# One more Strassen unit in the last gate pair, a shorter lead at its end, other accumulator banks for two groups, and another place for the last two quarter transposes of x1

## The chip, the cores and the metric

The kernel runs on one core of a Trainium2 chip. It is one launch that computes one decoder layer for 256 tokens. The metric is the device time of that launch in microseconds (us), the median over several runs, each of them one execution.

## The reference, cut to what matters

```python
h = rmsnorm(x, norm_mix_g);  u = h @ w_in              # D = 2048, 256 tokens
c_g, b_g, xa, za, q, fl, iv, og, ga, gb = split(u)
ya = b_g * causal_dwconv3(c_g * xa, conv_w) * silu(za)
o  = hgrn2_chunked(silu(q), (1 - lb) * sigmoid(-fl), iv, log_f)
yb = o * lax.rsqrt(mean(o * o) + EPS) * hg_norm_g * silu(og)
m  = sigmoid(ga) * (ya @ w_a_out) + sigmoid(gb) * (yb @ w_b_out)
x  = x + m @ w_o
gate = sigmoid(rmsnorm(x, ple_norm_g) @ w_ple_gate)    # 2048 x 2048
x  = x + gate * (p @ w_ple_proj)
return rmsnorm(x, final_norm_g)
```

All operands are fp32. The change touches the product with `w_o`, the product with `w_ple_gate` (`w_pg` in the kernel), and one scaling in the HGRN2 branch.

## The kernel before

**Products.** The 256 tokens are two halves `t` of 128 (`NT`), and the contraction of 2048 is 16 blocks of 128 (`KT`). An fp32 operand is split in two parts, hi and lo, and a product is three matmuls: hi by hi, hi by lo, lo by hi. A weight chunk of two blocks by 512 columns is one *step*. `split` (lines 143 to 173) writes the hi part of a step's weights on ScalarE (`whi`, L166) and the lo part on VectorE (`wlo`, L167), 128x1024 each, and the matmuls of the step then use them. A full step is 12 matmuls of 128x512 (L1258, or L1280 where two groups are a pair). The raw weights come on the queue of SP (`raw`, 3 buffers, 1 MB each). The split parts live in a ring of ten.

**Groups.** A group is 512 output columns. The stages run in this order: the projections with `w_in`, the merge gates, then `w_o` (a pair `OO` with columns 0 and 1, then `O` with j = 2 and j = 3), then `w_pg` (`PG0`, the pair `GP` with groups 1 and 2, then the last group, `PG3`). A pair follows a *program*, a tuple of units. The unit `(0, c)` takes group 0 at chunks c and c + 1, `(1, c)` the same for group 1, `(2, c)` takes chunk c for both groups (two steps, 8 products), and `("S", c)` takes chunk c for both groups by Strassen's form: 7 products, 4 steps. Three of these steps split 128x1024 and one 128x512, the latter from `t2`. After the first step of such a unit `combine_weights` (L181, L184, L185, VectorE) makes its sums of weights in place. `forms` makes the matching sums of the activations. The banks of a pair are put together by `sums` (L845), which for `GP` feeds `gated` (L1014 sigmoid on ScalarE; L1017 `t*pw` and L1018 `xs+t` on VectorE; L1026 a multiplication by `gfin_t` on GpSimd).

**The turn of x1.** When a group of `w_o` is done, `ep_o` adds it to the residual (L845, `xs`), copies it into another order on ScalarE (L947), and has it transposed by `turned`: four DMA writes to DRAM (L346, `turn<-t`), one DMA read (L350, `t<-turn`), then, `lag` steps later in the program, a 32x32 transposition on VectorE (L354). For the quarters j = 2 and 3 `put` then splits it into `xh` (ScalarE, L310, four instructions) and `xl` (VectorE, L311, four). Quarter j = 3 is chunks 6 and 7 of every product with `w_pg`. `lag` is 6 for j = 1 and otherwise 2.

**Order.** Each engine works through its instructions in the order of its own list. A scheduler makes the lists from the order in which the program issues the instructions and from what they depend on, with `issue_after` as a hint and `keep_in_program_order` to hold an instruction. The splits are issued `ahead(pos)` steps before the matmuls that use them; from the last stage on this lead grows from 3 by one every 3 steps, to 8 at most (line 1251). Epilogues are generators, of which `advance` takes one `yield` at each step. The positions in `tied` get an `issue_after` on the split before.

**Banks.** PSUM has four banks with the tag `g` and four with the tag `s`. A plain group uses two `g` banks, a pair four `g` and four `s`.

**The end.** The last group (from line 1446) does its half t = 0 with 128x512 matmuls, and t = 1 twice with 128x256; all its splits are issued during t = 0.

The program of the last pair:

```python
LATE = (0, 4), ("S", 0), (0, 6), ("S", 1), (2, 3), ("S", 2), (1, 4), (1, 6)
```

## Time and profile before

| | us |
|---|---|
| median of 3 runs (808.6 to 808.78) | 808.68 |
| the profiled execution, its own time | 809.07 |
| its span, first to last instruction | 807.3 |
| PE busy | 798.0 (99%) |
| VectorE (DVE) busy | 685.1 (85%) |
| ScalarE (ACT) busy | 492.1 (61%) |
| GpSimd (POOL) busy | 95.4 (12%) |
| mean granted clock of TensorE | 0.996 |

A row of the timeline has the start in us, the duration in us, the engine, the line, the operation, output<-inputs by the program's names, partitions x elements and type, and the number of instructions put together in the row; in brackets stands the idle time ahead of it and what ended it. Matmuls overlap: the duration of one is longer than the distance to the next, which is 0.2266 us for a 128x512 fp32 matmul here, so time lost on PE is read from the starts. SPq is the queue of SP. The timeline cuts the names of tiles shorter than the lists of instructions below do: `t` is `t4_...` or `t2_...`, `xl` is `xl_1039`.

### The profile page before, as it was taken

To read this page: it belongs to the slowest core of one execution; us is meant where nothing else is said; L and a number is where in the kernel's file an instruction comes from. 1 tells how busy PE (TensorE), PEld (TensorE's weight loads), DVE (VectorE), ACT (ScalarE), POOL (GpSimd) and SP (SyncE) were. 2 spreads that over 40 slices of the span, in tenths; PEclk is the share of its full clock that TensorE was granted. 3 is DMA by queue.
4 is the path that set the end of the run, shared out by engine and by line. 5 is a ranking of instruction groups with operands and counts; after the bars stand their busy time and mean duration, and the time that the engine had idled before them with its cause. 6 is when DMAs were issued, how large, how long until landed. Compare 5 with 4: busy or idle time off the path is not lost.

```text
span 807.3 us, 11113 instructions
## 1 busy us (share of the span) xinstructions
PE 798.0 (99%) x4169; PEld 662.3 (82%) x4169; DVE 685.1 (85%) x798; ACT 492.1 (61%) x662; POOL 95.4 (12%) x74
## 2 busy tenths in 40 slices
PE   9999999999999999999999999999999999999995
PEld 7888888888888888888888888888888888887885
DVE  5968897966779987978998998998998988859995
ACT  6967565575656665586674564564565556746562
POOL 0000145300000054300001000000100000002032
PEclk9999999999999999999999999999999999999998
DMA  9899855747676755667584775775875669877542
GB/s 345 295 335 319 268 174 203 237 167 241 240 261 190 261 183 201 209 211 257 189 307 158 227 275 171 239 264 179 275 266 196 208 246 348 327 236 281 205 173 104
DMA packets 50309, 191.20 MB, mean 237 GB/s; under 512 B 5712, under 2 KB 15184, under 8 KB 36304
## 3 DMA queue, kind: packets, MB, share of 16 engines
q1 hardware_dynamic: 50112, 190.24, 68.4%
q8 instruction: 32, 0.52, 0.2%
q10 hardware_dynamic: 144, 0.26, 0.1%
q14 instruction: 21, 0.17, 0.1%
HBM read 175.80 MB, written 14.68 MB: 236 GB/s over the span
## 4 chain that ended last, share of the span: by engine, by line
PE 82%; DVE 10%; issue 2%; DMA 2%; ACT 2%; SPq 0%; POOL 0%; ACTq 0%; POOLq 0%; DVEq 0%
PE g L1258 48%; PE g L1280 25%; PE s L1280 6%; DVE wlo L167 5%; DMA raw<-in_w_pg 2%; ACT whi L166 1%; DVE raw L181 1%; DMA raw<-in_w_o 1%; PE s L1258 1%; PE s L504 1%; DVE t L845 1%; PE s L1131 1%; DVE t L184 1%; DVE t L1017 0%; DVE t L354 0%
## 5 line engine op out<-in xcount | busy, mean ns | idle before, releaser
L167 DVE TENSOR_TENSOR wlo<-raw,whi 128x1024 fp32r<-128x1024 f32 (+1 forms) x320 | 390.2, 1243 | 92.2 <-ACT whi L166 89.4
L166 ACT ACTIVATE whi<-raw 128x1024 fp32r<-128x1024 f32 (+1 forms) x320 | 325.8, 1047 | 175.8 <-PE g L1258 98.3
L1258 PE MATMUL g<-whi,xl 128*128 128x512 f32 (+1 forms) x464 | 177.1, 382 | 0.3 <-DVE xl L311 0.3
L1258 PE MATMUL g<-whi,xh 128*128 128x512 f32 (+1 forms) x464 | 177.4, 383 | 0.0
L1258 PE MATMUL g<-wlo,xh 128*128 128x512 f32 (+1 forms) x464 | 177.1, 382 | 0.0
L1280 PE MATMUL g<-whi,xl 128*128 128x512 f32 x316 | 122.9, 389 | 0.0
L1280 PE MATMUL g<-wlo,xh 128*128 128x512 f32 x316 | 122.9, 389 | 0.0
L1280 PE MATMUL g<-whi,xh 128*128 128x512 f32 x316 | 122.6, 389 | 0.0
L1258 PEld LDWEIGHTS g<-whi,xl 128*128 128x128 f32 x464 | 87.2, 188 | 17.6 <-DVE xl L311 0.8
L1258 PEld LDWEIGHTS g<-whi,xh 128*128 128x128 f32 x464 | 87.2, 188 | 17.0 <-ACT xh L310 0.3
L1258 PEld LDWEIGHTS g<-wlo,xh 128*128 128x128 f32 x464 | 87.3, 188 | 16.8
L166 ACT ACTIVATE whi<-t 128x512 fp32r<-128x512 f32 x25 | 15.8, 632 | 92.1 <-DVE t L184 92.1
L1280 PEld LDWEIGHTS g<-whi,xl 128*128 128x128 f32 x316 | 59.3, 188 | 12.4
L1280 PEld LDWEIGHTS g<-whi,xh 128*128 128x128 f32 x316 | 59.3, 188 | 12.3
L1280 PEld LDWEIGHTS g<-wlo,xh 128*128 128x128 f32 x316 | 59.3, 188 | 12.3
L927 POOL TENSOR_TENSOR t<-ga,gb 128x512 f32<-128x512 f32 x6 | 10.6, 1790 | 188.0 <-issue 118.1
L181 DVE TENSOR_TENSOR raw<-raw 128x1024 f32<-128x1024 f32 x25 | 31.5, 1261 | 0.6
L1258 PE MATMUL g<-whi,yaTh 128*128 128x512 f32 (+1 forms) x74 | 28.2, 388 | 0.0
L1258 PE MATMUL g<-wlo,yaTh 128*128 128x512 f32 (+1 forms) x74 | 27.9, 383 | 0.0
L1258 PE MATMUL g<-whi,yaTl 128*128 128x512 f32 (+1 forms) x74 | 27.9, 383 | 0.0
L1258 PE MATMUL g<-whi,mh 128*128 128x512 f32 x64 | 24.8, 391 | 0.1
L1258 PE MATMUL g<-whi,ml 128*128 128x512 f32 x64 | 24.9, 389 | 0.0
(309 smaller groups left out, 1117.0 us busy)
## 6 DMA issues: line engine op xcount, KB each, us to landing
raw<-in_w_in SPq DMA_DIRECT2D x68, 1024.0 KB, 5.0
raw<-in_w_in SPq DMA_DIRECT2D x37, 512.0 KB, 5.1
raw<-in_w_o SPq DMA_DIRECT2D x12, 1024.0 KB, 6.5
raw<-in_w_pg SPq DMA_DIRECT2D x12, 1024.0 KB, 6.4
raw<-in_w_in SPq DMA_DIRECT2D x38, 256.0 KB, 5.1
turn<-t SPq DMA_DIRECT2D x72, 128.0 KB, 2.8
t<-turn SPq DMA_DIRECT2D x18, 512.0 KB, 5.2
raw<-in_w_a SPq DMA_DIRECT2D x8, 1024.0 KB, 5.6
```

What stands on the lines that cost most here:

```text
L166: a = nc.scalar.activation(out=hi[:, s], in_=src[:, s], func=AF.Copy)
L167: v = nc.vector.tensor_tensor(out=lo[:, s], in0=src[:, s], in1=hi[:, s].bitcast(F32), op=ALU.subtract)
L181: nc.vector.tensor_tensor(out=b[:, 0:4:3, :], in0=b[:, 0:3:2, :], in1=b[:, 3:4, :].to_broadcast([P, 2, CW]), op=ALU.subtract)
L184: nc.vector.tensor_tensor(out=t2, in0=b[:, 2, :], in1=b[:, 0, :], op=ALU.add)
L504: nc.tensor.matmul(heads(bk)[r, h, c if at is None else slice(at, at + 32)], key(h)[:, r], query(h)[:, c], start=True, stop=True, tile_pos ...
L845: nc.vector.tensor_tensor(out=out, in0=x, in1=y, op=ALU.add)
L927: (nc.vector if j == 3 else nc.gpsimd).tensor_tensor(out=spread(m, t), in0=blocks(ga[:, s]), in1=blocks(gb[:, s]), op=ALU.add)
L1131: nc.tensor.matmul(wb[:m, :n], *ones, start=True, stop=True)
L1258: nc.tensor.matmul(psum, a, b, start=first and n == 0, stop=last and n == 2)
L1280: nc.tensor.matmul(banks[name], x, y[:, s], start=k == total[name] and i == 0, stop=k == 1 and i == 2)
```

## The change

`LATE` gets four Strassen units: `(2, 3)` goes, `("S", 3)` comes, and the form of x1's quarter 1 (`So1`) is twice as wide. The lead of the splits begins to grow two steps earlier, but up to two steps past the last Strassen unit it is bounded (`united`). From the fifth to the eleventh step after `late` (the first step of `PG0`) the matmuls are kept in program order, and the first instruction of `combine_weights` gets an `issue_after` on the last `put` of quarter 3. `tied` reaches into `PG0`. The lags of the four quarters are 2, 6, 6 and 5. `O` with j = 2 and the half t = 0 of the last group take `s` banks. In `ep_f` with j = 1 four scalings (L407) go from VectorE to ScalarE, with one more `yield` behind them.

```diff
--- before.py
+++ after.py
@@ -44,7 +44,7 @@
 INNER = (0, 4), ("S", 0), (0, 6), ("S", 1), (2, 3), ("S", 2), (1, 4), (1, 6)
 FRONT = (0, 2), (0, 4), (0, 6), ("S", 0), (1, 2), ("S", 1), (1, 4), (1, 6)
 OUT = (0, 4), ("S", 0), (1, 4), ("S", 1), (2, 3), ("S", 2), (0, 6), (1, 6)
-LATE = (0, 4), ("S", 0), (0, 6), ("S", 1), (2, 3), ("S", 2), (1, 4), (1, 6)
+LATE = (0, 4), ("S", 0), (0, 6), ("S", 1), (1, 4), ("S", 2), ("S", 3), (1, 6)
 
 
 PRM_GMIX, PRM_GPLE, PRM_GHG, PRM_LB, PRM_CONV = 0, 16, 32, 40, 48
@@ -178,9 +178,12 @@
         if more(pos) in ("inner", "first"):
             pool, tag, n = "tmp1", ("both", "aoff")[unit_of[pos] // 2 % 2], 1
         t2 = half[unit_of[pos]] = pools[pool].tile([P, CW], F32, tag=tag, bufs=n, name=nm("t2"))
-        nc.vector.tensor_tensor(
-            out=b[:, 0:4:3, :], in0=b[:, 0:3:2, :], in1=b[:, 3:4, :].to_broadcast([P, 2, CW]), op=ALU.subtract
-        )
+        with ExitStack() as order:
+            for i in state.pop("puts", ()):
+                order.enter_context(tc.issue_after(i))
+            nc.vector.tensor_tensor(
+                out=b[:, 0:4:3, :], in0=b[:, 0:3:2, :], in1=b[:, 3:4, :].to_broadcast([P, 2, CW]), op=ALU.subtract
+            )
         nc.vector.tensor_tensor(out=t2, in0=b[:, 2, :], in1=b[:, 0, :], op=ALU.add)
         nc.vector.tensor_tensor(out=b[:, 1, :], in0=b[:, 1, :], in1=t2, op=ALU.subtract)
 
@@ -245,14 +248,14 @@
         return of_kind(kind)[0] + sum(4 if u == "S" else 2 for u, _ in program[: n + 1]) - 1
 
     tied = []
-    opening = last_unit("G0", OPENING)
+    opening, united = last_unit("G0", OPENING), last_unit("GP", LATE)
     g0 = range(of_kind("G0")[0] - 4, opening + 1)
     tied.append(range(g0[0], opening + 12))
     gates = range(opening + 5, of_kind("OO")[0] + 2)
     closing = last_unit("OO", OUT)
     last = range(gates[-1] + 1, closing + 1)
     outer = range(closing + 6, of_kind("O")[-1] + 1)
-    tied.append(range(last[0] - 4, outer[-1] + 1))
+    tied.append(range(last[0] - 4, late + 10))
     inner = [of_kind(kind) for kind in ("QV", "VG")]
     inner = range(inner[0][0] - 3, inner[0][-1] + 1), range(inner[1][0] - 6, inner[1][-1] + 1)
 
@@ -307,10 +310,11 @@
             nc.scalar.activation(out=hi, in_=src, func=AF.Copy)
             nc.vector.tensor_tensor(out=lo, in0=src, in1=hi.bitcast(F32), op=ALU.subtract)
         else:
-            nc.scalar.activation(out=hi, in_=src, func=AF.Identity, scale=scale)
-            nc.vector.scalar_tensor_tensor(
+            a = nc.scalar.activation(out=hi, in_=src, func=AF.Identity, scale=scale)
+            v = nc.vector.scalar_tensor_tensor(
                 out=lo, in0=src, scalar=scale, in1=hi.bitcast(F32), op0=ALU.mult, op1=ALU.subtract
             )
+            return a.ins, v.ins
 
 
     def rsqrt_of(ss, n, width, tag):
@@ -404,6 +408,11 @@
         one, low = (state[n][:, j * 4 : j * 4 + 4] for n in ("oml", "lbm"))
         for h in range(4):
             s = slice(h * T, (h + 1) * T)
+            if j:
+                nc.scalar.activation(
+                    out=sg[:, s], in_=sg[:, s], func=AF.Identity, scale=one[:, h : h + 1], bias=low[:, h : h + 1]
+                )
+                continue
             nc.vector.tensor_scalar(
                 out=sg[:, s], in0=sg[:, s], scalar1=one[:, h : h + 1], scalar2=low[:, h : h + 1],
                 op0=ALU.mult, op1=ALU.add,
@@ -416,7 +425,8 @@
             )
         yield
         yield
-
+        if j:
+            yield
 
         lf, last = t4(), sc(8, "lfl", 2)
         lv, fv = segments(lf), segments(sg)
@@ -945,7 +955,7 @@
             d = xs[:, t, j * CW : (j + 1) * CW]
             add(d, d, psum[t])
             nc.scalar.activation(out=spread(x1, t), in_=blocks(d), func=AF.Copy)
-        turn = turned(x1, 6 if j == 1 else 2)
+        turn = turned(x1, (2, 6, 6, 5)[j])
         next(turn)
         yield
         junk = t4()
@@ -970,8 +980,9 @@
             yield from forms("x1T", form_tiles(pools["tmp3"], f"So{j}", len(chunks)), r, chunks)
             return
         for c in range(4):
-            put(state["x1T"], j * 4 + c, x1[:, c * T : (c + 1) * T], gain(PRM_GPLE, j * 4 + c))
+            state["splits"] = put(state["x1T"], j * 4 + c, x1[:, c * T : (c + 1) * T], gain(PRM_GPLE, j * 4 + c))
         if j == 3:
+            state["puts"] = state["splits"]
             tot = sc(2, "tot2", 1)
             nc.vector.tensor_reduce(
                 out=tot, in_=state["ss2"].rearrange("p (t j) -> p t j", t=NT),
@@ -1248,14 +1259,19 @@
         at, n = more(pos + LEAD), 0
         while n < len(MORE[at]) and more(pos + LEAD + n + 1) == at and (at == "gates" or more(pos + LEAD - 2 * n) == at):
             n += 1
-        return LEAD + min(max(pos - late - 4, 0) // 3, 5) + n
+        far = LEAD + min(max(pos - late - 2, 0) // 3, 5) + n
+        if pos <= united + 2:
+            far = min(far, united + 4 - pos if pos < united else LEAD + 1)
+        return far
 
     def product(psum, op, k, t, hi, lo, first, last, which=(0, 1, 2)):
 
         oh, ol = (x[:, k, t * P : (t + 1) * P] for x in op)
         for n in which:
             a, b = ((oh, hi), (oh, lo), (ol, hi))[n]
-            nc.tensor.matmul(psum, a, b, start=first and n == 0, stop=last and n == 2)
+            m = nc.tensor.matmul(psum, a, b, start=first and n == 0, stop=last and n == 2)
+            if late + 5 <= pos < late + 12:
+                tc.keep_in_program_order(m)
 
     def ask_ahead():
 
@@ -1277,9 +1293,11 @@
                 banks[name] = bank("g" if type(name) is tuple else "s")
             k = left[name]
             for i, (x, y) in enumerate(((xh, hi), (xh, lo), (xl, hi))):
-                nc.tensor.matmul(
+                m = nc.tensor.matmul(
                     banks[name], x, y[:, s], start=k == total[name] and i == 0, stop=k == 1 and i == 2
                 )
+                if late + 5 <= pos < late + 12:
+                    tc.keep_in_program_order(m)
             left[name] -= 1
 
         def tile_of(k, t):
@@ -1400,7 +1418,7 @@
                 load_projection(1 + c[0] // 2)
             continue
         if c == 0:
-            psum = [bank("s" if kind == "PP" and j > 1 else "g") for _ in range(NT)]
+            psum = [bank("s" if kind == "PP" and j > 1 or kind == "O" and j == 2 else "g") for _ in range(NT)]
         hi, lo = parts.pop(pos)
         for i in range(2):
             k = 2 * c + i
@@ -1444,7 +1462,7 @@
 
     nlast = len(steps) - last_group
     for t, halves in ((0, (0, 1)), (1, (0,)), (1, (1,))):
-        bk, n = bank("g"), CW // 2
+        bk, n = bank("g" if t else "s"), CW // 2
         for c in range(nlast):
             if done < len(steps):
                 split(done)
```

What moves, at three places. First PE, at chunk 6 of `PG0` (banks `g_1118` and `g_1119`), the first that reads x1's quarter 3; `g_1151` and `g_1152` are banks of the pair `GP`. Before:

```order
L1280 MATMUL g_1152_6478<-wlo_1137_6399,xh_1038_5825 128x512
L1280 MATMUL g_1152_6478<-whi_1136_6398,xl_1039_5826 128x512
L1280 MATMUL g_1151_6474<-whi_1136_6398,xh_1038_5825 128x512
L1280 MATMUL g_1151_6474<-wlo_1137_6399,xh_1038_5825 128x512
L1258 MATMUL g_1118_6292<-whi_1130_6360,xh_1038_5825 128x512
L1258 MATMUL g_1118_6292<-wlo_1131_6361,xh_1038_5825 128x512
L1258 MATMUL g_1119_6293<-whi_1130_6360,xh_1038_5825 128x512
L1258 MATMUL g_1119_6293<-wlo_1131_6361,xh_1038_5825 128x512
L1280 MATMUL g_1151_6474<-whi_1136_6398,xl_1039_5826 128x512
L1280 MATMUL g_1152_6478<-whi_1136_6398,xh_1038_5825 128x512
L1258 MATMUL g_1118_6292<-whi_1130_6360,xl_1039_5826 128x512
L1258 MATMUL g_1119_6293<-whi_1130_6360,xl_1039_5826 128x512
```

Now, where the same chunk starts:

```order
L1272 MATMUL g_1118_6292<-whi_1126_6344,xh_1038_5825 128x512
L1272 MATMUL g_1118_6292<-wlo_1127_6345,xh_1038_5825 128x512
L1272 MATMUL g_1118_6292<-whi_1126_6344,xl_1039_5826 128x512
L1272 MATMUL g_1119_6293<-whi_1126_6344,xh_1038_5825 128x512
L1272 MATMUL g_1119_6293<-wlo_1127_6345,xh_1038_5825 128x512
L1272 MATMUL g_1119_6293<-whi_1126_6344,xl_1039_5826 128x512
L1272 MATMUL g_1118_6292<-whi_1126_6344,xh_1038_5825 128x512
```

Before, the chunk's hi·hi and hi·lo matmuls of one bank and then the other were mixed with matmuls of the pair; now the chunk runs from its first matmul on in the order of the program, three matmuls for one bank and three for the other.

Second VectorE, around the transposition of quarter 3 (`t4_1114`) and its four `xl`. Before:

```order
L319 TENSOR_SCALAR r2v_1128_6356<-tot2_1127_6354 128x2
L167 TENSOR_TENSOR wlo_1134_6381<-raw_1113_6271,whi_1133_6380 128x1024
L167 TENSOR_TENSOR wlo_1137_6399<-raw_1123_6326,whi_1136_6398 128x1024
L354 STREAM_TRANSPOSE t4_1126_6344<-t4_1114_6273 128x4x8x32
L167 TENSOR_TENSOR wlo_1140_6417<-raw_1123_6326,whi_1139_6416 128x1024
L167 TENSOR_TENSOR wlo_1142_6433<-raw_1132_6376,whi_1141_6432 128x1024
L311 SCALAR_TENSOR_TENSOR xl_1039_5826<-t4_1126_6344,prm_t_84,xh_1038_5825 128x256 x4
L181 TENSOR_TENSOR raw_1132_6376<-raw_1132_6376 128x2x512
L184 TENSOR_TENSOR t2_1143_6436<-raw_1132_6376 128x512
L185 TENSOR_TENSOR raw_1132_6376<-raw_1132_6376,t2_1143_6436 128x512
```

Now:

```order
L167 TENSOR_TENSOR wlo_1133_6383<-raw_1123_6326,whi_1132_6382 128x1024
L167 TENSOR_TENSOR wlo_1135_6387<-raw_1123_6326,whi_1134_6386 128x1024
L987 TENSOR_REDUCE tot2_1138_6414<-ss2_1036_5822 128x2
L323 TENSOR_SCALAR r2v_1139_6416<-tot2_1138_6414 128x2
L167 TENSOR_TENSOR wlo_1142_6421<-raw_1128_6360,whi_1141_6420 128x1024
L358 STREAM_TRANSPOSE t4_1137_6404<-t4_1114_6273 128x4x8x32
L314 SCALAR_TENSOR_TENSOR xl_1039_5826<-t4_1137_6404,prm_t_84,xh_1038_5825 128x256 x4
L184 TENSOR_TENSOR raw_1128_6360<-raw_1128_6360 128x2x512
L187 TENSOR_TENSOR t2_1143_6424<-raw_1128_6360 128x512
L188 TENSOR_TENSOR raw_1128_6360<-raw_1128_6360,t2_1143_6424 128x512
```

The two splits that stood between the transposition and `xl`, and a third between them and the combination of weights, are no longer there: one split precedes the transposition (it was two behind `r2v`), and the combination follows `xl` directly.

At the same place the queue of SP, with the writes (`turn_1115`) and the read of quarter 3. Before:

```order
L131 DMA raw_1108_6237<-in_w_pg 128x2048
L131 DMA raw_1113_6271<-in_w_pg 128x2048
L346 DMA turn_1115_6278<-t4_1114_6273 32x4x256 x4
L131 DMA raw_1123_6326<-in_w_pg 128x2048
L350 DMA t4_1114_6273<-turn_1115_6278 128x1024
L119 DMA raw_1132_6376<-in_w_pg 128x1024
L121 DMA raw_1132_6376<-in_w_pg 128x512 x2
L1209 DMA pw_1135_6396<-kept_26_224 128x1024
```

Now:

```order
L131 DMA raw_1107_6227<-in_w_pg 128x2048
L131 DMA raw_1113_6271<-in_w_pg 128x2048
L1220 DMA pw_1131_6380<-kept_26_224 128x1024
L131 DMA raw_1123_6326<-in_w_pg 128x2048
L350 DMA turn_1115_6278<-t4_1114_6273 32x4x256 x4
L119 DMA raw_1128_6360<-in_w_pg 128x1024
L121 DMA raw_1128_6360<-in_w_pg 128x512
L354 DMA t4_1114_6273<-turn_1115_6278 128x1024
L121 DMA raw_1128_6360<-in_w_pg 128x512
L131 DMA raw_1136_6402<-in_w_pg 128x2048
```

The load of `pw` stands ahead of the turn's writes rather than behind the weights, and so does one load of raw weights of 1 MB; behind the writes the read now stands behind two pieces of a Strassen unit's weights.

Third VectorE at the end of the last pair: `wlo_1222` and `wlo_1224` were the splits of chunks 6 and 7 of the last group, L1017 and L1018 are the second gate of the pair. Before:

```order
L1017 TENSOR_TENSOR t4_1208_6712<-t4_1208_6712,pw_1166_6540 128x512
L167 TENSOR_TENSOR wlo_1220_6770<-raw_1205_6703,whi_1219_6769 128x1024
L1018 TENSOR_TENSOR xs_5814<-xs_5814,t4_1208_6712 128x512
L167 TENSOR_TENSOR wlo_1222_6788<-raw_1212_6727,whi_1221_6787 128x1024
L167 TENSOR_TENSOR wlo_1224_6804<-raw_1212_6727,whi_1223_6803 128x1024
L845 TENSOR_TENSOR t4_1209_6713<-t4_1209_6713,g_1174_6561 128x512
L845 TENSOR_TENSOR t4_1209_6713<-t4_1209_6713,g_1202_6683 128x512
L1017 TENSOR_TENSOR t4_1209_6713<-t4_1209_6713,pw_1189_6630 128x512 x2
L1018 TENSOR_TENSOR xs_5814<-xs_5814,t4_1209_6713 128x512 x2
L1035 TENSOR_TENSOR t4_1228_6894<-t4_1228_6894,pw_1218_6767 128x256
```

Now these splits are `wlo_1229` and `wlo_1231`:

```order
L855 TENSOR_TENSOR t4_1214_6747<-t4_1214_6747,g_1174_6560 128x512
L1029 TENSOR_TENSOR xs_5814<-xs_5814,t4_1213_6746 128x512
L855 TENSOR_TENSOR t4_1214_6747<-t4_1214_6747,g_1200_6670 128x512
L167 TENSOR_TENSOR wlo_1226_6827<-raw_1210_6725,whi_1225_6826 128x1024
L1028 TENSOR_TENSOR t4_1214_6747<-t4_1214_6747,pw_1191_6635 128x512 x2
L1029 TENSOR_TENSOR xs_5814<-xs_5814,t4_1214_6747 128x512 x2
L167 TENSOR_TENSOR wlo_1229_6846<-raw_1217_6781,whi_1228_6845 128x1024
L167 TENSOR_TENSOR wlo_1231_6856<-raw_1217_6781,whi_1230_6855 128x1024
L1046 TENSOR_TENSOR t4_1233_6904<-t4_1233_6904,pw_1219_6793 128x256
```

They stood ahead of the second gate's four instructions and now stand behind them.

## The prediction

> **What bounds the kernel now.** I read the page's busy times first, then the chain of waits, then the starts of PE's matmuls with the timeline.
>
> ```profile
> PE 798.0 (99%) x4169; PEld 662.3 (82%) x4169; DVE 685.1 (85%) x798; ACT 492.1 (61%) x662; POOL 95.4 (12%) x74
> PE 82%; DVE 10%; issue 2%; DMA 2%; ACT 2%; SPq 0%; POOL 0%; ACTq 0%; POOLq 0%; DVEq 0%
> ```
>
> PE is busy 99% of the span of 807.3 us, so the time falls only by matmuls that go or by places where the distance between starts exceeds 0.2266 us. VectorE is at 85%, the next engine to bind, and it holds 10% of the chain. Three places in PE's list stand where the change reaches. At the turn from `PG0` to the pair:
>
> ```profile
> 728.87 0.62 PE L1280 MATMUL g<-whi,xh 128*128 128x512 f32 x2
> ...
> 730.46 0.39 PE L1280 MATMUL g<-wlo,xh 128*128 128x512 f32 x1
> ...
> 732.79 0.73 PE L1258 MATMUL g<-whi,xl 128*128 128x512 f32 x2 [0.35 <-DVE xl L311]
> 733.36 0.39 PE L1258 MATMUL g<-whi,xh 128*128 128x512 f32 x1
> ```
>
> From 730.46 to 733.36 lie nine starts, 2.90 us where 9 x 0.2266 = 2.04 would do: 0.86 us lost, waiting for x1's quarter 3. At the start of `O` with j = 2, PE and VectorE:
>
> ```profile
> 669.12 0.39 PE L1258 MATMUL g<-whi,ml 128*128 128x512 f32 x1
> ...
> 670.38 0.39 PE L1258 MATMUL g<-whi,mh 128*128 128x512 f32 x1
> 664.95 0.68 DVE L845 TENSOR_TENSOR t<-t,s 128x512 f32<-128x512 f32 x1
> ...
> 668.84 0.68 DVE L845 TENSOR_TENSOR t<-t,g 128x512 f32<-128x512 f32 x1
> ```
>
> 1.26 us over four starts (0.91) is 0.35 lost: the second `g` bank is still being read by VectorE until about 669.5. In the pair `VG`, PE and VectorE:
>
> ```profile
> 268.05 0.39 PE L1280 MATMUL g<-whi,xh 128*128 128x512 f32 x1
> ...
> 269.26 0.39 PE L1280 MATMUL s<-whi,form 128*128 128x512 f32 x1
> 236.85 0.41 DVE L407 TENSOR_SCALAR t<-t,lc,lc 128x256 f32<-128x256 f32 x1
> ...
> 247.05 3.50 DVE L167 TENSOR_TENSOR wlo<-raw,whi 128x1024 fp32r<-128x1024 f32 x3 [1.36 <-ACT whi L166]
> ```
>
> 1.21 over four starts is 0.31 lost at a Strassen unit whose combined weights come late from VectorE, which 20 us earlier still had 1.36 us idle.
>
> **The parts, costed.** (1) `("S", 3)` for `(2, 3)` makes 7 products of 8. That is three matmuls fewer, 3 x 0.2266 = **-0.68**. No matmul is added elsewhere, and the forms are VectorE's and ScalarE's work ahead of the stage.
>
> (2) Quarter 3. Its chain on VectorE and ScalarE:
>
> ```profile
> 727.72 1.23 DVE L167 TENSOR_TENSOR wlo<-raw,whi 128x1024 fp32r<-128x1024 f32 x1 [4.26 <-ACT whi L166]
> 728.86 1.24 DVE L354 STREAM_TRANSPOSE t<-t 128x1024 f32<-128x1024 f32 x1
> 730.02 2.32 DVE L167 TENSOR_TENSOR wlo<-raw,whi 128x1024 fp32r<-128x1024 f32 x2
> 732.25 1.67 DVE L311 SCALAR_TENSOR_TENSOR xl<-t,prm_t,xh 128x256 fp32r<-128x256 f32 x4
> 733.84 1.22 DVE L181 TENSOR_TENSOR raw<-raw 128x1024 f32<-128x1024 f32 x1
> 730.23 1.69 ACT L310 ACTIVATE xh<-t,prm_t 128x256 fp32r<-128x256 f32 x4
> 712.53 1.06 ACT L166 ACTIVATE whi<-raw 128x1024 fp32r<-128x1024 f32 x1 [1.38 <-PE g L1258]
> ...
> 715.21 0.62 ACT L947 ACTIVATE t<-xs 128x512 f32<-128x512 f32 x1
> ```
>
> Two splits (730.02 to 732.25) stand between the transposition and `xl`, though VectorE had been idle 4.26 before. In the changed list both are gone from there. The chain starts when `O` with j = 3 ends, at 712.5 (the row of ScalarE that PE released). VectorE has quarter 2 behind it by then, so the two additions are done early, and on ScalarE three hi splits (3 x 1.0) and two copies (0.62) end about 716.8. The writes leave at 716.8 to 718.2. What follows is read from the times from issue to landing, in this order of the writes at 679.0 and those at 695.1, both behind a load of weights, of the read at 702.4 and that of quarter 3 at 722.2, and of a load of 1 MB at 752.8:
>
> ```profile
> DMA to landing us min/median/max: 6.7/6.9/7.2
> ...
> DMA to landing us min/median/max: 5.8/6.0/6.1
> ...
> DMA to landing us min/median/max: 3.9/3.9/3.9
> ...
> DMA to landing us min/median/max: 5.6/5.6/5.6
> ...
> DMA to landing us min/median/max: 5.0/5.0/5.0
> ```
>
> The writes now follow `pw` and a 1 MB load on the queue. That load leaves when a raw buffer is free, about 715.6, and by the 5.0 lands at 720.6; the writes come in behind it, the last near 721.9 (3.7 after its issue; 5.8 to 7.2 is what the other two needed, with more of the load ahead of them). The read leaves at 721.95, with only 0.75 MB ahead of it, and lands at 721.95 + 3.9 = 725.8, or with the 5.6 at 727.6. The split ahead of the transposition has its weights behind the writes (issue near 718.3, 5.0 to land, 1.0 on ScalarE, 1.1 on VectorE) and ends at 725.4. So the transposition goes at 725.85, 3.0 earlier than before. After 1.16 for it the first `xh` is ready near 727.6, and `xl` ends 3.4 after its start (1.16, 0.6 to the first `xh`, 1.67), at **729.25**, where it was 733.84. PE, in program order, wants the first `xh` at 728.87, where the first row of PE above stands. The margin is 1.3 us; it is gone at a landing of 727.1. Taken: the whole wait goes, **-0.84** (the gaps of single rows; 0 to -0.86, and a loss if the read is later, rival C).
>
> (3) `O` with j = 2 in `s` banks: the pair's first `s` bank has its read at 664.95, four us before the `g` bank's at 668.84, so the wait goes: **-0.35** (0 to -0.35).
>
> (4) `VG`: four L407 of 0.41, 1.64 together, leave VectorE's list ahead of the combination. The 1.36 of idle time at 247.05 swallows most of that, 0.28 is left, and the unit's splits on ScalarE, which takes the scalings, come no earlier. Taken half of what is lost, **-0.16** (0 to -0.31). ScalarE, at 61%, hides the scalings in its own idle time; uncovered they would cost no more than the 0.28.
>
> (5) What it costs. VectorE gets a combination, a half split and one full split in `GP`. By these rows:
>
> ```profile
> 735.09 0.69 DVE L184 TENSOR_TENSOR t<-raw 128x512 f32<-128x512 f32 x1
> ...
> 736.43 1.22 DVE L167 TENSOR_TENSOR wlo<-raw,whi 128x1024 fp32r<-128x1024 f32 x1
> 737.56 0.69 DVE L167 TENSOR_TENSOR wlo<-t,whi 128x512 fp32r<-128x512 f32 x1
> 738.16 1.22 DVE L167 TENSOR_TENSOR wlo<-raw,whi 128x1024 fp32r<-128x1024 f32 x1
> 739.30 1.29 DVE L1017 TENSOR_TENSOR t<-t,pw 128x512 f32<-128x512 f32 x2
> ```
>
> The combination is 736.43 - 733.84 = 2.59, the half split 738.16 - 737.56 = 0.60, a full split 739.30 - 738.16 = 1.14: **4.33 us** more between the first combination and the splits of the last group. The second gate's four instructions also move ahead of the splits of chunks 6 and 7. The stretch before, and its slowed rows:
>
> ```profile
> 733.84:788.52 54.68, 52.08 (x56) 1.00 0.54 196
> ...
> 745.23 2.20 DVE L181 TENSOR_TENSOR raw<-raw 128x1024 f32<-128x1024 f32 x1
> 747.47 1.67 DVE L184 TENSOR_TENSOR t<-raw 128x512 f32<-128x512 f32 x1
> ...
> 781.41 2.35 DVE L167 TENSOR_TENSOR wlo<-raw,whi 128x1024 fp32r<-128x1024 f32 x2
> ...
> 785.15 2.17 DVE L1017 TENSOR_TENSOR t<-t,pw 128x512 f32<-128x512 f32 x2 [0.20 <-ACT t L1014]
> 742.48 6.10 POOL L1026 TENSOR_TENSOR xs<-xs,gfin_t 128x512 f32<-128x512 f32 x2 [18.46 <-ACT t L1019]
> 779.99 6.18 POOL L1026 TENSOR_TENSOR xs<-xs,gfin_t 128x512 f32<-128x512 f32 x2 [31.40 <-ACT t L1019]
> ...
> 788.75 1.29 POOL L1026 TENSOR_TENSOR xs<-xs,gfin_t 128x512 f32<-128x512 f32 x1 [2.59 <-ACT t L1019]
> ```
>
> VectorE was busy 52.08 of 54.68 us from the first combination to the end of the second gate. The new list has all of that and 4.33 more, less the 1.14 of chunk 7, before chunk 6's split ends: 55.3. Two places in the 52.08 are slower than the same operation elsewhere, while GpSimd works (its rows at 742.48 and 779.99): 2.20 for 1.22 and 1.67 for 0.69, 1.96 together, and 2.17 for 1.29, 0.88. Without the second, which hangs on the meeting of two instructions at the end, it is 54.4 us, so chunk 6 is split at 729.25 + 54.4 = 783.65; with it at 784.5; without either at 781.7. PE needs it 240 matmuls behind 728.87 (243 in the list of before, less 3), at 728.87 + 240 x 0.2266 = 783.25, the lo part one matmul later, at 783.5. The wait is 0, 0.15 or 1.0; I take **+0.3**, nearest to the middle one, since the first slowing comes in a stretch that keeps its order. Half of the 2.6 us in which VectorE was idle, on top of the 1.0, is the upper bound, 2.3 (that idle time was spent waiting for ScalarE, which a VectorE that is behind no longer does). Chunk 7 follows 1.14 later, where PE needs six matmuls, 1.36, so nothing queues behind it, and the tail after t = 1 is untouched.
>
> **The sum.** -0.68 - 0.84 - 0.35 - 0.16 + 0.30 = -1.73. Against the profiled execution, 809.07, that is 807.35 with a span of 805.6; the median of the runs, 808.68, lies 0.39 below that execution, and 808.68 - 1.73 = 806.95, so **807.0**.
>
> **The rivals.** *B, VectorE becomes the bound in the last group.* For it: 85% busy, 4.33 us more in a stretch with 2.6 idle, the gate ahead of chunks 6 and 7. Against it: quarter 3 is out 4.6 us earlier. With chunk 6 late by 1.0 to 2.3 the time is 806.65 + 1.0 to 2.3, 807.7 to 809.0, likeliest 808.3. A read that takes 5.6 also ends here: PE waits 0.5, VectorE starts 1.8 later and chunk 6 is 1.6 late, -2.03 + 0.5 + 1.6, near 808.7.
>
> *E, GpSimd holds VectorE up at both gates.* A row of 1.29 is what GpSimd's multiplication takes alone (788.75). If each of a gate's two multiplications stops VectorE for its whole length, that is 2.6 in place of the 0.88 or nothing at the second gate, chunk 6 is late by 1.7 more than taken, and the time is 808.7. For it: 2.17 at 785.15. Against it: the two splits at 781.41 took 2.35, as the two at 730.02 did (2.32), while GpSimd was at work, and it was GpSimd's pair that stretched, to 6.18.
> The Trainium skill, page "SBUF — State Buffer", section "Who interferes with whom", states that a VectorE instruction with two SBUF inputs contends with a GpSimd instruction that reads SBUF, and that whoever issues first holds the shared pair for the whole instruction while the other "fully blocks". By that rule the time would be that of E; the trace agrees at 745.23 and 785.15 and shows nothing of it at 781.41.
>
> *C, quarter 3 lands late.* The writes take 7.2, as at 679, and the read 5.6: landing at 729.7, past the 727.1 from which PE waits. PE, held in program order, has nothing else there and stands 2.65 us; `xl` ends at 733.1, hardly earlier than before, and chunk 6, for which PE then comes 2.65 later, is 1.5 late. The sum is -0.68 - 0.35 - 0.16 - 0.84 + 2.65 + 1.5 = +2.1, **810.8**; it is the case on the other side, even at a landing of 727.6 and slower by over 0.2% from 729.3 on. For it: the writes now stand behind two transfers. Against it: the load ahead of them leaves 1.2 earlier than they do, and the read at 702.4 took 3.9.
>
> *D, the stalls stay.* Only the matmuls go; `VG` and `O` wait as before for something else, and what quarter 3 saves chunk 6 loses: 808.68 - 0.68 = **808.0**.
>
> **How the numbers follow.** Chances: the forecast 0.58, with a range of its own from 806.5 (all gains at their ends, nothing for chunk 6) to 807.6; B 0.16; E 0.08; C 0.11; D 0.07. About 0.2%, 1.6 us, is what a measurement of this kernel can tell from no change, so faster begins below 807.06. Of the forecast's 0.58, 0.49 lie below that and 0.09 above; B, E and D are no change (0.31), C is slower: faster 0.49, same 0.40, slower 0.11. The range, 806.3 to 809.1, takes in all but C and a little beyond the lower end.
>
> **What would show it.** The new profile has a place for each step: PE's starts even at 0.2266 through chunks 6 and 7 of `PG0` (else C); the read of quarter 3 landing before 727.1 and `xl` ending near 729; no gap at the second bank of `O` with j = 2; less than 0.31 lost in `VG`; and in the last group, at chunk 6 of t = 0, a gap of PE of about 0.3 released by `wlo`. A gap there above 1 us is B, or E if the gate's rows on VectorE stand at 2.2 beside GpSimd's. A gap of PE elsewhere, above all at `("S", 3)`, whose combination and splits come one behind the other on VectorE, would make the prediction wrong in a way that I have not priced.

## The result, and the profile after

| | before | changed |
|---|---|---|
| median of 6 runs, us | 808.71 (808.29 to 809.38) | 812.82 (811.77 to 813.6) |
| profiled execution, span, us | 809.07, 807.3 | 812.6, 810.8 |

The ratio is 1.0052, with a 95% interval of 1.0041 to 1.0062: the change makes the kernel 4.1 us slower, where 1.7 us faster was forecast. Ratios, here and below, leave out the few executions at a visibly lower granted clock (one of `lead_after_units`, 1521.5 us at 0.836, and two of `units_bank`, 1003.0 and 889.5 us); medians take them in.

The page's busy times and chain of the changed kernel:

```profile
PE 798.4 (98%) x4165; PEld 662.5 (82%) x4166; DVE 690.9 (85%) x799; ACT 495.6 (61%) x668; POOL 91.6 (11%) x74
PE 92%; DVE 3%; DMA 2%; issue 1%; ACT 1%; SPq 0%; ACTq 0%; POOLq 0%; POOL 0%
```

PE is busy 798.4 us with three matmuls fewer (four by the records), 0.4 more than before: some matmuls took longer. The timeline of PE at chunk 6 of the last group, half t = 0, shows where; under it stand those of VectorE and of GpSimd:

```profile
783.51 0.39 PE L1272 MATMUL s<-whi,xh 128*128 128x512 f32 x1
786.87 0.50 PE L1272 MATMUL s<-wlo,xh 128*128 128x512 f32 x1 [2.96 <-DVE wlo L167]
787.20 0.47 PE L1272 MATMUL s<-whi,xl 128*128 128x512 f32 x1
787.47 0.63 PE L1272 MATMUL s<-whi,xh 128*128 128x512 f32 x1
787.89 0.63 PE L1272 MATMUL s<-wlo,xh 128*128 128x512 f32 x1
...
790.89 0.40 PE L1272 MATMUL s<-whi,xl 128*128 128x512 f32 x1
```

```profile
780.96 1.22 DVE L167 TENSOR_TENSOR wlo<-raw,whi 128x1024 fp32r<-128x1024 f32 x1
782.09 2.38 DVE L1028 TENSOR_TENSOR t<-t,pw 128x512 f32<-128x512 f32 x2
784.39 1.28 DVE L1029 TENSOR_TENSOR xs<-xs,t 128x512 f32<-128x512 f32 x2
785.60 3.43 DVE L167 TENSOR_TENSOR wlo<-raw,whi 128x1024 fp32r<-128x1024 f32 x2
```

```profile
781.29 2.03 POOL L1037 TENSOR_TENSOR xs<-xs,gfin_t 128x512 f32<-128x512 f32 x1 [2.62 <-ACT t L1030]
785.91 4.25 POOL L1037 TENSOR_TENSOR xs<-xs,gfin_t 128x512 f32<-128x512 f32 x2 [2.59 <-ACT t L1030]
```

The hi part of chunk 6 is there at 783.51. The lo part comes 3.35 us later (3.13 lost), since its split (785.60, done 786.8) stands behind the second gate's four instructions, the first of them held up beside GpSimd. PE had waited once before, at chunk 5, for the split at 780.96 (0.37 lost from 781.78 on). After the long gap the matmuls follow each other at 0.43 us rather than 0.2266. The windows of PE say why; the column behind the busy time is the granted clock:

```profile
783.97:787.38 3.41, 0.51 (x2) 1.00 0.00 0
787.38:790.80 3.42, 3.42 (x9) 0.50 0.00 0
790.80:794.21 3.41, 3.41 (x28) 1.00 0.00 0
```

From 787.4 to 790.8, 3.4 us, TensorE had half its clock, beginning half a microsecond after work had resumed. Between 787.20 and 790.89 lie nine distances, 3.69 us for 2.04: 1.65 lost. At the first matmul of chunk 6 in `PG0` the chain of quarter 3 did what was forecast, nearly:

```profile
726.71 1.25 DVE L358 STREAM_TRANSPOSE t<-t 128x1024 f32<-128x1024 f32 x1 [0.51 <-DMA t<-turn]
728.52 1.69 DVE L314 SCALAR_TENSOR_TENSOR xl<-t,prm_t,xh 128x256 fp32r<-128x256 f32 x4 [0.57 <-ACT xh L313]
730.13 1.22 DVE L184 TENSOR_TENSOR raw<-raw 128x1024 f32<-128x1024 f32 x1
```

```profile
727.88 0.39 PE L1272 MATMUL g<-whi,xl 128*128 128x512 f32 x1
728.54 0.50 PE L1272 MATMUL g<-whi,xh 128*128 128x512 f32 x1 [0.28 <-ACT xh L313]
728.88 0.40 PE L1272 MATMUL g<-wlo,xh 128*128 128x512 f32 x1
```

The read landed at 726.7 rather than 725.8, and PE lost 0.55 there at two matmuls (0.66 and 0.34 for two of 0.2266), 0.64 from 725 to 735 in all, where 0.86 were lost before. Summed over the two profiled executions: matmuls -0.68, quarter 3 -0.22, the gaps at `O` and in `VG` gone -0.66, chunk 5 +0.37, chunk 6 +3.13, the matmul behind it +0.11, half clock +1.65, together +3.70; the last matmul starts 3.59 later (802.52 for 798.93).

### The profile page after: what moved, and what is told of

The parts are those of the page before. It is cut to its first block, busy times and chain, and to the rows that moved or that the text cites. A ratio compares the mean times of both kernels' runs of the same rounds, so it can differ in the third digit from the quotient of the medians.

```text
span 810.8 us, 11116 instructions
## 1 busy us (share of the span) xinstructions
PE 798.4 (98%) x4165; PEld 662.5 (82%) x4166; DVE 690.9 (85%) x799; ACT 495.6 (61%) x668; POOL 91.6 (11%) x74
## 4 chain that ended last, share of the span: by engine, by line
PE 92%; DVE 3%; DMA 2%; issue 1%; ACT 1%; SPq 0%; ACTq 0%; POOLq 0%; POOL 0%
PE g L1272 48%; PE g L1296 30%; PE s L1296 8%; PE s L1272 4%; DVE wlo L167 1%; PE s L514 1%; DMA turn<-t 1%; DMA raw<-in_w_pg 1%; ACT whi L166 1%; PE s L1142 1%; DMA t<-turn 1%; DVE t L855 0%; DVE t L1028 0%; PE s L647 0%; PE s L670 0%
## 5 line engine op out<-in xcount | busy, mean ns | idle before, releaser
L1272 PE MATMUL g<-whi,xh 128*128 128x512 f32 (+1 forms) x448 | 171.3, 383 | 0.3 <-ACT xh L313 0.3
L1272 PE MATMUL g<-whi,xl 128*128 128x512 f32 (+1 forms) x448 | 171.0, 382 | 0.0
L1272 PE MATMUL g<-wlo,xh 128*128 128x512 f32 (+1 forms) x448 | 170.9, 382 | 0.0
L1296 PE MATMUL g<-whi,xh 128*128 128x512 f32 x310 | 120.1, 389 | 0.0
L1272 PEld LDWEIGHTS g<-whi,xh 128*128 128x128 f32 x448 | 84.2, 188 | 16.9 <-ACT xh L313 0.7
L1272 PEld LDWEIGHTS g<-whi,xl 128*128 128x128 f32 x448 | 84.2, 188 | 16.4 <-DVE xl L314 0.2
L1272 PEld LDWEIGHTS g<-wlo,xh 128*128 128x128 f32 x448 | 84.2, 188 | 16.0
L1296 PEld LDWEIGHTS g<-whi,xh 128*128 128x128 f32 x310 | 58.2, 188 | 12.1
L1296 PEld LDWEIGHTS g<-whi,xl 128*128 128x128 f32 x310 | 58.2, 188 | 12.1
L1296 PEld LDWEIGHTS g<-wlo,xh 128*128 128x128 f32 x310 | 58.2, 188 | 12.0
L1272 PE MATMUL g<-whi,ybTh 128*128 128x512 f32 x64 | 24.9, 389 | 0.0
L1272 PE MATMUL g<-wlo,ybTh 128*128 128x512 f32 x64 | 24.9, 389 | 0.0
```

The source lines that it names most:

```text
L1272: m = nc.tensor.matmul(psum, a, b, start=first and n == 0, stop=last and n == 2)
L1296: m = nc.tensor.matmul(banks[name], x, y[:, s], start=k == total[name] and i == 0, stop=k == 1 and i == 2)
```

## The experiments

All ran beside the kernel before, whose median was 807.9 to 808.3 there. All are edits of the changed kernel unless the text says otherwise.

**The bound on the lead, lifted behind the last unit** (`lead_after_units`):

```diff
-        if pos <= united + 2:
-            far = min(far, united + 4 - pos if pos < united else LEAD + 1)
+        if pos < united:
+            far = min(far, united + 4 - pos)
```

> The changed kernel with the bound on the lead lifted as soon as the last Strassen unit is done (the bound holds only below it). In VectorE's list the splits of chunks 6 and 7 of the last group then stand ahead of the second gate's four instructions again. Theory (the order at the end: chunk 6's split waits behind the gate, PE stands 3.1 us for it, and TensorE's clock is lower for 3.4 us afterwards because PE stood): the gate took 3.5 us of VectorE ahead of chunk 6 (782.09 to 785.60), so the split ends more than 3.5 us earlier, PE's gap at chunk 6 goes, the clock stays at 1.00, and the time is 812.8 - 3.1 - 1.8 = 807.9. Rival 1 (the added work makes VectorE late wherever chunk 6 stands): a gap of 1 us or more stays in the last group or moves ahead to an earlier chunk, 809.5 or more. Rival 2 (the lower clock belongs to the new bank or another cause, not to the gap): the gap goes and the clock still falls, 809.7.

Measured: 807.71 beside 808.16, ratio 0.999 (0.9978 to 1.0002). Run again with more rounds, as `lead_after_units_b`:

> The kernel with the bound on the lead lifted as soon as the last Strassen unit is done, once more, for a tighter interval and an undisturbed profile. Theory as before: no gap of PE in the last group, clock 1.00 through it, 3 to 5 us below the changed kernel. Against the kernel before: 0.68 for the matmuls and up to 0.84 for quarter 3, of which the changed kernel's own profile shows 0.3 gained, so 0.7 to 1.5 us faster, ratio 0.998 to 0.999. If the 0.35 at O with j = 2 and the 0.31 in VG were losses of every execution of the kernel before, it would be 1.6 to 2.2 us, ratio 0.9973 to 0.998.

Measured: 807.71 beside 807.92, ratio 0.9999 (0.999 to 1.0008). VectorE's timeline of that run; chunk 6's split is the one at 777.93, chunk 7's that at 782.60, and the second gate follows:

```profile
777.93 1.22 DVE L167 TENSOR_TENSOR wlo<-raw,whi 128x1024 fp32r<-128x1024 f32 x1
...
782.60 1.22 DVE L167 TENSOR_TENSOR wlo<-raw,whi 128x1024 fp32r<-128x1024 f32 x1
783.74 1.28 DVE L855 TENSOR_TENSOR t<-t,g 128x512 f32<-128x512 f32 x2
785.21 2.17 DVE L1028 TENSOR_TENSOR t<-t,pw 128x512 f32<-128x512 f32 x2 [0.19 <-ACT t L1025]
```

PE has no gap in the last group and the clock stays whole. These two lines of the change cost the 4 to 5 us: the bound keeps the last group's splits of chunks 4 to 7 back until its own matmuls are issued, with the gate ahead of them. Both rivals fall. Against the kernel before nothing measurable is left.

**Three units as before, all else changed** (`three_units`): `LATE` with `(2, 3)`.

> The changed kernel with the three Strassen units of before, all else changed. Theory: chunk 6's split stands ahead of the second gate in this list and VectorE has 4.33 us less to do, so there is no gap in the last group and the clock stays; the gains at quarter 3, at O with j = 2 and in VG stay (0.3, 0.35, 0.31) and the three matmuls come back (0.68): 808.7 - 0.96 = 807.8. Rival (the shorter lead itself, or the bank of the last group, costs the time, not the unit): 811 or more with the gap still there.

Measured: 808.06, ratio 0.9998 (0.9988 to 1.0007), no gap in the last group. So unit and bound make the loss together; with three units the bound leaves chunk 6 ahead of the gate. The gain of 0.96 did not come: quarter 3's `xh` was 1.1 us late in this execution, and the two other terms (0.35 and 0.31) were no losses of the kernel, as `before_again` below shows.

**The four units alone, on the kernel before** (`units_alone`), and with the last group's first half in an `s` bank too (`units_bank`):

> The kernel before with the four Strassen units as its only edit: lead, lags, banks, scalings and order as before. Three matmuls fewer, 4.33 us more on VectorE. Theory (the units can be paid for where the splits of the last group keep their place ahead of the gate): all of the known gaps of the kernel before stay, chunk 6 of the last group ends its split at 782.6 + 4.3 less about 2 us of idle time, 785 by the clock of before, where PE needs it at 784.4: a gap of 0 to 0.8 and a time of 808.0 to 808.8. Rival (the fourth unit's 4.33 us alone make VectorE the bound): a gap above 2 us in the last group, 811 or more. Rival (the longer lead of before holds up the combination of the fourth unit): a gap of PE at that unit, 809 or more, with none in the last group.

> The kernel before with the four Strassen units and, for the half t = 0 of the last group, an s bank in place of a g bank: two edits. With the units alone PE stood 0.9 us at the first matmul of the last group, and 1.2 us at the fourth unit. Theory (the first of these is the g bank, which VectorE was still reading for the gate until 777): that gap goes, the other stays, and the time falls by 0.9 from the units alone, a ratio of 1.0014 for 1.0025. Rival (VectorE is late by then, and the next split takes the place of the bank): a gap of 0.5 us or more a few matmuls later in the last group, no gain.

Measured: 810.31, ratio 1.0025 (1.0016 to 1.0034), and 810.34, ratio 1.002 (1.0011 to 1.003). PE of the first, at the fourth unit and where the last group begins:

```profile
767.16 0.50 PE L1280 MATMUL s<-wlo,So1h 128*128 128x512 f32 x1 [0.52 <-DVE wlo L167]
...
777.25 0.50 PE L1258 MATMUL g<-whi,xh 128*128 128x512 f32 x1 [0.73 <-DVE t L845]
```

and of the second:

```profile
767.54 0.50 PE L1280 MATMUL s<-wlo,So1h 128*128 128x512 f32 x1 [0.53 <-DVE wlo L167]
...
787.16 0.50 PE L1258 MATMUL s<-wlo,xh 128*128 128x512 f32 x1 [0.47 <-DVE wlo L167]
```

The bank's wait goes (1.06 lost there with the matmuls behind it) and a wait for VectorE's next late split takes its place at 787 (0.76): the rival was right as to the mechanism. The two ratios cannot tell no gain from the 0.9 us that the theory forecast, since its 1.0014 lies within the interval; the profiles show 0.3. My range for the units alone, 808.0 to 808.8, was too low: VectorE is late at the fourth unit already. The gap there is the one that the second rival names (809 or more), but the last group has one too, and its cause was not shown to be the lead. VectorE's first combination starts at 732.94 in this run and at 730.13 in the changed kernel, which has no gap at that unit.

**GpSimd's multiplication left out for the first gate** (`no_gain_1`), **one addition of the second gate left out** (`one_sum_less`), **chunk 6's lo part written three times** (`two_more_splits`):

```diff
+            if j == 1:
+                continue
             nc.gpsimd.tensor_tensor(out=d, in0=d, in1=state["gfin"][:, j * CW : (j + 1) * CW], op=ALU.mult)
```

> The changed kernel without the final gain's multiplication on GpSimd for columns 512 to 1023, so these columns of the output lack the gain. Theory (VectorE's first t*pw of the second gate, 1.78 us for 0.68, was held for 1.1 us by GpSimd's multiplication of the first gate): the row becomes 0.68, chunk 6's split ends 1.1 us earlier, PE's gap at chunk 6 goes from 3.1 lost to 2.0. If the clock falls only after a stand of about 3 us it stays at 1.00, and the time is 812.8 - 1.1 - 1.8 = 809.9; if any gap lowers it, 811.7. Rival (GpSimd and VectorE don't hold each other, the slow row has another cause): row and time as in the changed kernel, 812.8.

> The changed kernel without the addition of the gate's product to the second half of the tokens for columns 1024 to 1535 (one instruction of VectorE, 0.60 us, ahead of chunk 6's split; these outputs lack it). Theory: the gap at chunk 6 is 0.6 shorter than in the changed kernel beside it, 2.4 to 3.0 from start to start. It lies between a gap of 2.28, after which the clock stayed, and one of 3.35, after which it was 0.50 for 3.4 us. If the clock falls by the length of the stand, with a point between these two, either may be seen here, and the time is 810.2 or so without the half clock and 811.9 with it; if a stand of any length brings it and the 2.28 was luck, 811.9.

> The changed kernel with the lo part of chunk 6 of the last group written three times rather than once on VectorE, the same values, so that PE waits 2 x 1.14 = 2.3 us longer there (or 1.1 more where GpSimd's multiplication falls in). Theory (the clock falls once for a stand above some 3 us, and comes back about 3.4 us after work resumes, whatever the length of the stand): gap 5.6 to 6.7, the clock again lower for 3 to 3.5 us and the loss from it again 1.8, time 815.1 to 816.2. Rival (the loss grows with the stand): 4 us and more at the lower clock, 816.5 or more.

Measured, one execution each: 809.67, 812.05 and 812.14. VectorE without the multiplication:

```profile
781.90 1.29 DVE L1028 TENSOR_TENSOR t<-t,pw 128x512 f32<-128x512 f32 x2
783.11 1.29 DVE L1029 TENSOR_TENSOR xs<-xs,t 128x512 f32<-128x512 f32 x2
```

The 2.38 becomes 1.29: GpSimd held VectorE up for 1.1 us. GpSimd's row at 781.29 in the changed kernel had itself been held up first, by the split at 780.96: 2.03 us for the 1.29 that it takes alone. PE in `no_gain_1`, and in the run with an addition less:

```profile
783.31 0.40 PE L1274 MATMUL s<-whi,xh 128*128 128x512 f32 x1
785.59 0.50 PE L1274 MATMUL s<-wlo,xh 128*128 128x512 f32 x1 [1.89 <-DVE wlo L167]
```

```profile
783.53 0.39 PE L1273 MATMUL s<-whi,xh 128*128 128x512 f32 x1
786.28 0.51 PE L1273 MATMUL s<-wlo,xh 128*128 128x512 f32 x1 [2.36 <-DVE wlo L167]
...
787.29 0.63 PE L1273 MATMUL s<-wlo,xh 128*128 128x512 f32 x1
787.72 0.63 PE L1273 MATMUL s<-whi,xl 128*128 128x512 f32 x1
```

After 2.28 us from start to start the clock stayed, after 2.75 it fell; the last section shows that the length of the stand is not what decides. With chunk 6 still later, windows of PE:

```profile
785.07:788.48 3.41, 0.00 (x0) 1.00 0.00 0
788.48:791.90 3.42, 2.90 (x7) 0.50 0.00 0
```

The gap is 4.3 there, since the scheduler drew matmuls of the next half ahead of it (so the time expected, 815.1, does not compare), and the half clock again lasts 3.4 us. It does not grow with the gap.

**Both kernels again, for a second profile** (`before_again`, `after_again`):

> The kernel before, unchanged, for a second profile of it. Theory 1 (the gap of 0.35 at O with j = 2 and that of 0.31 in VG belong to the kernel): both stand there again, at the same matmuls. Theory 2 (they are chance of one execution, as the run with the four units alone, whose program is the same up to there, has neither): one or both are missing, and so two of the gains that the sum counted are not the edits'. Gap of quarter 3: 0.86 in both.

> The changed kernel, unchanged, for a second profile on the chip of the other runs. Theory (order at the end, the gate and GpSimd ahead of chunk 6's split, then the half clock): a gap of 3.0 to 3.6 us from start to start at the second matmul of chunk 6 in the last group, ended by VectorE's wlo, the clock at 0.50 for 3.4 us right after it, and 811.8 to 813.6 us, a ratio to before of 1.004 to 1.006. Rival (the half clock is an accident of one execution): the gap without it, 810.8.

Measured: 808.36, and 811.91 with a ratio of 1.0049 (1.0031 to 1.0067). The changed kernel has the same gap (3.38) and 0.43 pitch again. The kernel before, PE in `VG` and at `O` with j = 2:

```profile
267.81 0.39 PE L1280 MATMUL g<-whi,xh 128*128 128x512 f32 x1
268.03 0.39 PE L1280 MATMUL g<-whi,form 128*128 128x512 f32 x1
268.26 0.39 PE L1280 MATMUL s<-whi,form 128*128 128x512 f32 x1
```

```profile
668.34 0.39 PE L1258 MATMUL g<-wlo,mh 128*128 128x512 f32 x1
668.57 0.39 PE L1258 MATMUL g<-whi,ml 128*128 128x512 f32 x1
668.79 0.39 PE L1258 MATMUL g<-whi,mh 128*128 128x512 f32 x1
```

No gap at either place: the 0.31 and the 0.35 were chance of the execution that was profiled first. At `O` VectorE's read of the `g` bank started at 667.83, where it was 668.84.

**Quarter 3 ahead of the pair's weights**, in two steps on the kernel with the bound lifted. `turn_first` issues the pair's loads after the writes; `read_first` puts the read right behind the writes too, the loads behind it, and sets the lag to 3:

```diff
-        if unit_of[pos] not in loaded and groups[steps[pos][0]][0] == "O":
+        if unit_of[pos] not in loaded and groups[steps[pos][0]][0] in ("O", "GP"):
```

> The same, and the pair's weight loads are issued after the writes of x1's quarter 3, so that no 1 MB load stands ahead of these writes on the queue. Theory (the gap at chunk 6 of PG0, 0.55 us lost in the changed kernel and more with three units, is the read landing at 726.7 to 727.2 since the writes land late behind the load): the writes land after 2.1 to 3.9 as in the kernel before, the read leaves 1 to 2 us earlier and lands before 726, the gap goes, and the time is 0.3 to 0.6 us below the run beside it. Rival (the read then stands behind that load, which takes its place in front): the read takes 5.6 as in the kernel before, the landing and the gap stay, no difference. Rival (the load, now 3 us later, holds up the pair's first splits): a gap of PE at the pair's first unit, 1 us or more slower.

> The changed kernel with the bound on the lead lifted after the last Strassen unit, and with x1's quarter 3 ahead of the pair's weights: the read of the turn is issued right behind its writes, the pair's loads wait until that read is issued, and the lag of the quarter is 3, so that VectorE transposes it and makes xl ahead of the two splits of the pair's first unit. Theory (in every variant so far the gap at chunk 6 of PG0 is the read, landing at 726.7 to 727.2 because a 1 MB load lies ahead of the writes or of the read): the writes land after 2.1 to 3.9, the read leaves near 719.8 and lands after 3.9 or less, by 723.7; the transposition starts near 724, the first xh is there by 726, before PE wants it at 728; the gap of 0.74 goes and the time is 0.7 us below the run without this edit (807.71 beside 807.92 for before), so 807.0 and a ratio near 0.9988. Rival (the weights, some 4 us later, come too late for the pair): a gap of PE at the pair's first or second unit, 808 or more.

Measured: 809.57, ratio 1.0018 (1.0009 to 1.0027), and 809.48, ratio 1.0015 (1.0006 to 1.0024). In the first the read did land earlier, at 725.5 (issued 721.4, 4.1 to landing), but two splits that wait for the delayed load stand ahead of the transposition (725.29 to 727.56), and PE lost 2.2 us at chunk 6 of `PG0`. That is the cause and the price of the second rival (the delayed load, 1 us or more), at another place than the pair's first unit. In the second, VectorE and PE:

```profile
724.05 1.25 DVE L358 STREAM_TRANSPOSE t<-t 128x1024 f32<-128x1024 f32 x1 [4.51 <-DMA t<-turn]
...
728.02 4.63 DVE L167 TENSOR_TENSOR wlo<-raw,whi 128x1024 fp32r<-128x1024 f32 x4 [0.46 <-ACT whi L166]
```

```profile
767.20 0.50 PE L1299 MATMUL s<-wlo,So1h 128*128 128x512 f32 x1 [0.95 <-DVE wlo L167]
...
787.37 0.50 PE L1275 MATMUL s<-wlo,xh 128*128 128x512 f32 x1 [0.33 <-DVE wlo L167]
```

The transposition starts at 724.05 as expected and PE has no gap at chunk 6 of `PG0`. But VectorE stood 4.51 us, and the splits behind the read could not have run in that time: their loads left at 721.24 and later and took 5.5 us or more to land. So the first combination starts at 732.68, where it was 730.52 with the bound lifted alone, and 34 us later PE waits at the fourth unit (1.37 and 0.57 from start to start) and again in the last group. The rival had the late weights right and the place wrong. That the late start is what comes back at the fourth unit is argued: `units_alone` (732.94) has that gap too, the two with a start at 730.13 and 730.52 have none, and in `turn_first` (732.28), where PE itself is 2.2 us late, there is none either. No version measurably faster than the kernel before was found.

## Why the prediction was wrong, step by step

- **The matmuls** (-0.68): held.
- **Quarter 3** (-0.84): the mechanism held, the margin of 1.3 us did not. The read landed at 726.7 instead of 725.8, its writes having landed 0.6 later and it having taken 4.1 for 3.9. And PE wanted the first `xh` at 728.11 rather than 728.87: the gaps at `O` and in `VG` did not stand ahead of it, which the sum counts as gains but the margin does not. The loss from 725 to 735 is 0.64 in this execution, 0.15 in `after_again`, 0.85 with the bound lifted, 1.31 with three units, and 0.55 on average over the seven profiles with this turn; the four with the turn of before lost 0.90 on average (0.85 to 1.03). So some 0.35 is gained, not 0.84. (Rival C's landing of 729.7 counts 7.2 us from the first write. Counted from the last write, issued at 718.2, with the 6.7 us that the shortest at 679 took, the read lands at 730.5.)
- **`O` and `VG`** (-0.35, -0.16): should not have been in the sum. They were read off one execution whose own time was 0.39 above the median; the second profile has neither.
- **The price on VectorE** is the step that failed: "I take **+0.3**, nearest to the middle one", with 2.3 as the upper end; measured 3.13, with 0.37 more at chunk 5. I gave three allowances one at a time and took the middle: the read (0.9 later, combination at 730.13 for 729.25), the meeting with GpSimd (1.1, which I left out as chance), and idle time (0.31, 0.26 and 0.20 waiting for ScalarE, which "a VectorE that is behind no longer does"). All three came, and 783.65 + 2.75 = 786.4 is nearly the 786.8 measured. I also priced the gate ahead of chunks 6 and 7 as given without asking which line put it there. It stands 3.5 us (782.09 to 785.60) ahead of the split, and the lifted bound showed that without it there is no wait.
- **The half clock** (1.65) stood in no term and no rival. Rival B named the place and the engine with a chance of 0.16, but its price was a wait alone and ended at 2.3. The Trainium skill, page "TensorE: Matmul & The Clock Gate", section "Part 1: The HAM clock gate (the "warmup" mystery)", says that an idle window of about 3.4 us halves the clock and that as long a busy one restores it. The 3.4 us at 0.50 agree; the idle window does not, for PE was busy for 0.51 us of the window ahead of the fall, and for 1.06 in `one_sum_less`.
- **Rival E** was right as to the mechanism and half its size: 1.1 us for one meeting. The Trainium skill, page "SBUF — State Buffer", section "Who interferes with whom", says that a VectorE instruction with two SBUF inputs contends with a GpSimd instruction that reads SBUF, and that issue order decides who blocks. The gate's two products at 2.38 us, and at 1.29 without the multiplication, agree.

## What to carry to other kernels

When an engine at 85% is given more work near the end, ask what stands directly ahead of the operand that PE needs next, and which rule put it there: here two lines on the lead cost more than the extra work itself. Add up the allowances for lateness along one chain rather than choosing the middle one, and price a stand of PE that can fill more than half of a 3.4 us window with the clock that it may lose afterwards (1.65 us here). A gap of a few tenths in one profiled execution is not a gap of the kernel until a second profile has it.

## What the runs showed of the hardware

- In these traces the granted clock went by windows, not by the length of a stand. In the changed kernel's trace it was whole for 781.65 us, half for 3.41 and whole for 17.07: 229, 1 and 5 times 3.413. In the other profiles the stretches at the whole clock are whole multiples too (795.3 us in `no_gain_1` is 233, 798.7 in `three_units` 234). Counted in these windows, in the thirteen profiles without that of `lead_after_units`, the clock fell at the end of every window in which PE was busy for 1.53 us or less (45%) and of none with 1.74 or more (51%); after a stand within the work it came back one window later (PE busy for 2.90 or more). `no_gain_1` has both cases, at its gap and at its end:

```profile
781.30:784.71 3.41, 2.40 (x11) 1.00 0.08 31
784.71:788.12 3.41, 2.53 (x11) 1.00 0.00 0
...
798.36:801.78 3.42, 1.53 (x13) 1.00 0.00 0
801.78:805.10 3.32, 0.00 (x0) 0.50 0.41 155
```

- Its stand of 2.28 us lay across two windows and cost nothing; after its last matmul (done 799.89) 1.89 us were enough. In the changed kernel nearly the whole stand lay in one window, and the window ended half a microsecond after work had resumed. The first window at the whole clock began 3.4 to 6.6 us after the start of the span, differently in each execution, so whether a stand of 2 or 3 us costs the clock is in part chance. Where between 45% and 51% the point lies is open.
- A multiplication on GpSimd that met the second gate cost VectorE 1.1 us once, near the 1.29 that it takes alone, and VectorE held GpSimd up as well: the two at 785.91 took 4.25 for 2 x 1.29.
